# Turning the second FFN's gated tiles with VectorE and a round trip through DRAM instead of TensorE

## The chip, the cores and the metric

The kernel runs on one core of one Trainium2 chip. The metric is the device time of one execution in microseconds (us). Engines are named as in the profile: PE (TensorE), DVE (VectorE), ACT (ScalarE), POOL (GpSimd) and SP (SyncE). SP, POOL and, with the change, ACT issue transfers, which all run on the core's sixteen DMA engines.

## The reference

One layer of a hybrid diffusion backbone with 256 latent and 256 context tokens, D = 2048: a SwiGLU FFN, a token mixer, a second SwiGLU FFN on the latent tokens alone, and a last RMSNorm. The change is in the second FFN:

```
def half_step_ffn(x, mod, i, g, w_up, w_down):
    h = adaln(x, g, mod, i)
    a, b = jnp.split(h @ w_up, 2, axis=-1)
    return x + 0.5 * mod[:, i + 2, None, :] * ((jax.nn.silu(a) * b) @ w_down)

    xl = half_step_ffn(xl, mod_l, 6, g_norm[l, 2], w_ffn2_up[l], w_ffn2_down[l])
return rms_norm(xl, g_final)
```

The hidden width is 5632 = 44 x 128. The kernel works on it in eleven blocks of 512 columns, n = 0 to 10.

## The kernel before

**Precision.** Every matrix product is three fp32r products: each operand is split into a rounded part `hi` (an ACT copy, L128) and the rest `lo` (a DVE subtraction, L129). A weight load of 1 MiB (128 x 2048, fp32) is split in two halves of 1024 columns (`split`, L120). `hi` and `lo` have four buffers each, so two loads are split ahead at most.

**The second FFN's main stage** runs from about 1996 to 2507 us of the profile. Two streams of work are woven by `sequence` (L2242), step by step:

- Steps "s" belong to `quad(n)`, n = 1 to 9. A quad makes one block's gated product, silu(a) * b, by seven products m = 0 to 6 of half the tokens and half the depth (a Strassen form). Each product takes two steps (q = 0, 1) of 12 matmuls. Products write PSUM banks X and Y.
- Steps "u" belong to the stream `units`: first block 10's up products (`up(LAST)`, 8 steps), then the down products of two blocks at a time (`down(n, n+1)`, 8 steps of 24 matmuls).

A quad after the first has 18 steps in this order, which the texts below number 1 to 18: m0 (1, 2), m1 (3, 4), u (5), m2 (6, 7), u (8), m3 (9, 10), m4 (11, 12), u (13), m5 (14, 15), u (16), m6 (17, 18). A step of the quad that follows has a dash: 4' is its fourth step.

**Weights of a quad.** The weights are not all plain loads; some are sums that the DMA engines form. `chain_[q]` is loaded by SP; `first(q)` (at m0) adds another part to it with an accumulating DMA on POOL's queue (`accum`, L740). That sum is what m2 splits at steps 6 and 7. More such sums feed m3 to m6 (`early`, `late_`, `chained`). The accumulation can be issued only when DVE has read the old contents (`lo`, L129). Plain loads go through three buffers `raw`, which SP fills as they come free.

**The gated tiles.** Each quad gives two tiles of 128 tokens x 512 columns: tile 0 in `c12` at the end of step 12, and tile 1 in `c21` at the end of step 18. The down product needs them with the columns on partitions. `wait_turn` puts them in the list `turn`; after each step `turned` (L2044) takes the first of them, if it is at least N_TURN = 2 steps old: four PE transposes through `ident` into a PSUM bank `tr` (L2058), then an ACT copy to `hid2h` (L2061) and a DVE subtraction to `hid2l` (L2063, which turns the sign). The first FFN does it another way (L833 to L845): DVE transposes 32 x 32 blocks, SP stores the tile to DRAM, and later it is fetched back from there in runs of 512 bytes (`hid_load`, L705).

**Order.** The instructions are placed on each engine by a scheduler that follows program order as far as operands are ready; those marked by `keep_in_program_order` (`pinned`) keep their order among themselves. Each engine and each issuing queue then goes through its own list in that order.

**The end.** After the last quad come the down products of blocks 8 and 9 (`down(8, 9)`), then those of block 10 with the last norm (`last2`).

Of the kernel before, what the change touches and what calls it, by code (L numbers as in the profile page):

```python
# [34 lines left out]

N_HID = 3

N_TURN = 2

PACE = (4, 2), (12, 13), (19, 19), (27, 28), (35, 37), (42, 44), (51, 51), (58, 54), (65, 61), (70, 70), (73, 76), (74, 85), (79, 96)  # L40
PACE += (86, 102), (92, 109), (98, 118), (100, 130), (103, 144), (106, 152), (109, 163), (112, 170), (128, 181)
# [17 lines left out]
def tile_layer(ctx: ExitStack, tc: tile.TileContext, I: dict, out: bass.AP):  # L59
# [681 lines left out]
    with pool(name="f1u", bufs=1) as f1u:  # L741
# [91 lines left out]
        def turned():  # L833

            if not turn:
                return
            n, t, ca, spare = turn.pop(0)
            if (n, t) == (NB - 1, 3):
                spare = chp.tile([P, CB], F32, tag="stg", name="stg")
            pinned(nc.vector.transpose(spare, ca))  # L840
            s, tt = divmod(t, 2)
            nc.sync.dma_start(hidd[n][2 * tt + s], spare)
# [1088 lines left out]
    with f2x:  # L1931
        def hid_tiles():

            return [f2.tile([P, FB, T], F32R, tag=g, name=g, bufs=N_HID) for g in ("hid2h", "hid2l")]
# [38 lines left out]
        xTcm.__exit__(None, None, None)  # L1973
        x2cm.__exit__(None, None, None)
        banks.close()
        ps["mm"] = ctx.enter_context(pool(name="ps2", bufs=4, space=PSUM))
        psx = ctx.enter_context(pool(name="psx", bufs=1, space=PSUM))
        ps["tr"] = ctx.enter_context(pool(name="pt2", bufs=2, space=PSUM))
        f2b = f2x.enter_context(pool(name="f2b", bufs=2))

        f3 = ctx.enter_context(pool(name="f3", bufs=1, side="right"))
# [59 lines left out]
        summed = set()  # L2041
        born, clock = {}, [0]

        def turned():  # L2044

            if not turn:
                return
            n, t, sa, sign = turn[0]
            if clock[0] < born[n, t] + N_TURN:
                return  # L2050
            if n not in hids:
                if n - 1 not in hids or len(hids) - len(summed) >= N_HID:
                    return
                hids[n] = hid_tiles()
            turn.pop(0)
            tb = tbank()
            for j in range(FB):
                nc.tensor.transpose(tb[:, j * P : (j + 1) * P], sa[:, j * P : (j + 1) * P], ident)  # L2058
            t3 = tb.rearrange("p (j c) -> p j c", j=FB)
            hh, hl = (x[:, :, t * P : (t + 1) * P] for x in hids[n])  # L2060
            nc.scalar.activation(hh, t3, AF.Copy, scale=sign)  # L2061
            if sign < 0:
                nc.vector.scalar_tensor_tensor(hl, t3, -1.0, hh.bitcast(F32), op0=ALU.mult, op1=ALU.subtract)  # L2063
            else:
                nc.vector.tensor_tensor(hl, t3, hh.bitcast(F32), op=ALU.subtract)
            done.add((n, t))

        done = set()

        def wait_turn(n, t, sa, sign):  # L2070
            turn.append((n, t, sa, sign))
            born[n, t] = clock[0]
            turn.sort(key=lambda x: x[:2])

        def ca_tile():
            return f2b.tile([P, CB], F32, tag="ca", name="ca", bufs=3)

        def quad(n):

            add = lambda o, x, y: nc.vector.tensor_tensor(o, x, y, op=ALU.add)  # L2080
            mul = lambda o, x, y: nc.vector.tensor_tensor(o, x, y, op=ALU.mult)
            B, g = {}, {}

            def p1():
# [25 lines left out]
            def c21():  # L2110
                add(g["a"], B["Y"], g["a"])
                nc.scalar.activation(g["a"], g["a"], AF.Silu)
                mul(g["a"], g["a"], g["y"])
                wait_turn(n, 1, g["a"], -1.0)

            def chained(ab, c):
                return lambda q: accum(chain_[q], part(n, ab, c + q))
# [62 lines left out]
        def up(n):  # L2180

            sab = []
            for ab in range(2):
                bs = [bank() for _ in range(2)]
                for u in range(4):
                    wt = load_split(part(n, ab, u))
                    for j in range(4):
                        k = 4 * u + j
                        w = slice(j * CB, (j + 1) * CB)
                        for t in range(2):  # L2190
                            tt = slice(t * P, (t + 1) * P)
                            mm3(bs[t], h2hi[:, k, tt], h2lo[:, k, tt], *wt(w), k == 0, k == KT - 1)
                    if u == 3:
                        for t in range(2):
                            if ab:
                                nc.vector.tensor_tensor(sab[t], sab[t], bs[t], op=ALU.mult)
                                wait_turn(n, t, sab[t], 1.0)
# [14 lines left out]

        def down(*ns):

            for cb in range(NCB):
                c = slice(cb * CB, (cb + 1) * CB)
                bs = [bank() for _ in range(2)]
                for n in ns:
                    assert (n, 1) in done or not n
                    wt = load_split(I["w_dn2"][n, cb])  # L2220
                    for t in range(2):
                        block(bs[t], n, wt, t, n == ns[0], n == ns[-1])
                    if n == ns[-1]:
                        for t in range(2):
                            a = acc2[:, t, c]
                            if not ns[0]:
                                nc.scalar.activation(a, bs[t], AF.Copy)
                            else:
                                nc.vector.tensor_tensor(a, a, bs[t], op=ALU.add)
                            if n == LAST - 1:  # L2230
                                half_gated(a, a, late["g8"][:, c])
                                accum(a, x2d[t * P : (t + 1) * P, c])
                        if cb == NCB - 1:
                            summed.update(ns)
                    yield

        def units():
            yield from up(LAST)
# [37 lines left out]
        drain(down(LAST - 2, LAST - 1))  # L2276

        def last2():

# [69 lines left out]
def _laid_out(a):  # L2349
# [30 lines left out]
    for n in "12":  # L2380
        up, dn = a[f"w_ffn{n}_up"][0], a[f"w_ffn{n}_down"][0]
        nf = dn.shape[0] // P
        up = up.reshape(KT, P, 2, nf, P)

        rest = up[:, :, :, FB:].reshape(4, 4, P, 2, nf // FB - 1, CB)
        m[f"w_up{n}b"] = asc(rest.transpose(4, 3, 0, 2, 1, 5).reshape(nf // FB - 1, 2, 4, P, 2048))
        first = up[:, :, :, :FB].transpose(3, 2, 1, 0, 4).reshape(-1, 2, P, 2048)
        m[f"w_up{n}"] = asc(first[NPRE:])
        pre = first[:NPRE].reshape(2 * NPRE, P, KT, P)
        loads = []  # L2390
        for k0, k1 in BLOCKS if n == "1" else BLOCKS2:
# [3 lines left out]
        rows = dn.reshape(NF // FB, FB, P, NCB, CB).transpose(0, 3, 2, 1, 4).reshape(NF // FB, NCB, P, 2048)  # L2395
        if n == "1":
            turned = dn.reshape(NF // FB, 4, FB, 32, NCB, CB).transpose(0, 4, 1, 3, 2, 5).reshape(NF // FB, NCB, P, 2048)
            rows = np.concatenate([rows[:1], turned[1:]])
        m[f"w_dn{n}"] = asc(rows)
    w = a["w_in"][0]  # L2400

# [32 lines left out]
```

## Time and profile before

| | us |
|---|---|
| median of 3 runs | 2590.29 |
| the 3 runs | 2586.33, 2590.29, 2592.44 |
| the profiled execution | 2588.91 |
| its span, first to last instruction | 2587.2 |

So 1.7 us of the profiled execution lie outside the span. How to read the profile: the page gives the busy time of each engine and a chain of what released what, followed back from the last instruction. The view of windows gives the busy time of each engine within a stretch, and then the granted PE clock, the mean busy share of the sixteen DMA engines and the rate in GB/s. The view of DMA queues gives, for each queue, packets, megabytes and the time that its packets took as a share of sixteen engines' time in the window; q0 is POOL's queue and q1 holds what SP issues. In a row of the timeline the bracket tells how long the engine sat idle before the instruction, and what it waited for.

### The profile page before, as it was taken

How to read it: one execution, taken by the hardware profiler on the slowest of the kernel's cores; microseconds unless marked ns; L12 is line 12 of the kernel's file. 1: busy time of each engine (PE TensorE's matmuls, PEld its weight loads, DVE VectorE, ACT ScalarE, POOL GpSimd, SP SyncE). 2: the span in 40 equal slices, each digit the busy share in tenths (PEclk: the TensorE clock that was granted, in tenths of full speed). 3: DMA queues.
4: the chain of work that ended last, by engine and by line, in shares of the span. 5: the costliest groups of instructions: out<-in, count | busy, mean ns of one | idle time of the engine just before them, and what ended most of it. 6: DMA issues, size and time to landing. Idle time of an engine off the chain costs nothing. (4 is left out here: it accounts for less than half of the span.)

```text
span 2587.2 us, 33868 instructions
## 1 busy us (share of the span) xinstructions
PE 2555.3 (99%) x12486; PEld 2124.7 (82%) x12486; DVE 2206.6 (85%) x2924; ACT 1405.5 (54%) x1798; POOL 221.9 (9%) x271
## 2 busy tenths in 40 slices
PE   8999999999999999999999999999999999999998
PEld 5788888888887878888889889888898888888886
DVE  7789888888888788888887888898889888898987
ACT  5454444444444455444454347466486676667763
POOL 0000000100010100010110000120000000000001
PEclk8999999999999999999999999999999999999999
DMA  9989999999999999999987897776768999999985
GB/s 392 355 214 275 265 290 277 262 292 281 276 285 282 255 236 246 213 221 231 231 242 268 295 315 242 237 282 212 267 233 246 275 277 283 278 286 278 273 248 171
DMA packets 153478, 684.70 MB, mean 265 GB/s; under 512 B 22872, under 2 KB 43864, under 8 KB 92000
## 3 DMA queue, kind: packets, MB, share of 16 engines
q1 hardware_dynamic: 123936, 490.64, 51.7%
q0 software_dynamic: 29376, 191.90, 37.3%
q8 instruction: 98, 1.61, 0.2%
q14 instruction: 68, 0.56, 0.1%
HBM read 664.59 MB, written 17.89 MB: 264 GB/s over the span
## 5 line engine op out<-in xcount | busy, mean ns | idle before, releaser
L128 ACT ACTIVATE hi<-raw 128x1024 fp32r<-128x1024 f32 (+2 forms) x488 | 504.5, 1040 | 401.2 <-PE mm L152 298.7
L129 DVE TENSOR_TENSOR lo<-raw,hi 128x1024 fp32r<-128x1024 f32 (+2 forms) x476 | 567.2, 1204 | 105.7 <-ACT hi L128 87.4
L128 ACT ACTIVATE hi<-chain 128x1024 fp32r<-128x1024 f32 x352 | 370.1, 1059 | 352.6 <-PE mm L152 199.3
L129 DVE TENSOR_TENSOR lo<-chain,hi 128x1024 fp32r<-128x1024 f32 x352 | 425.2, 1219 | 92.5 <-ACT hi L128 81.2
L152 PE MATMUL mm<-hi,hhi 128*128 128x512 f32 (+3 forms) x1024 | 390.7, 382 | 0.0
L152 PE MATMUL mm<-lo,hhi 128*128 128x512 f32 (+3 forms) x1024 | 387.7, 379 | 1.9 <-DVE lo L129 1.8
L152 PE MATMUL mm<-hi,hlo 128*128 128x512 f32 (+3 forms) x1024 | 386.6, 378 | 0.0
L208 DVE SCALAR_TENSOR_TENSOR junk<-sraw,cBh 128x1024 fp8e5<-128x1024 f32 x192 | 234.3, 1220 | 40.5 <-DMA sraw<-in_w_mt 39.0
L152 PEld LDWEIGHTS mm<-lo,hhi 128*128 128x128 f32 x1024 | 192.8, 188 | 37.0 <-DVE lo L129 4.0
L152 PEld LDWEIGHTS mm<-hi,hlo 128*128 128x128 f32 x1024 | 193.0, 189 | 32.0
L152 PEld LDWEIGHTS mm<-hi,hhi 128*128 128x128 f32 x1024 | 192.9, 188 | 32.2 <-ACT hi L128 0.3
L129 DVE TENSOR_TENSOR lo<-ra,hi 128x1024 fp32r<-128x1024 f32 x104 | 126.2, 1222 | 25.6 <-ACT hi L128 21.7
L128 ACT ACTIVATE hi<-ra 128x1024 fp32r<-128x1024 f32 x104 | 110.1, 1062 | 64.0 <-PE mm L152 34.2
L152 PE MATMUL mm<-lo,hid2h 128*128 128x512 f32 x352 | 137.1, 389 | 0.0
L152 PE MATMUL mm<-hi,hid2h 128*128 128x512 f32 x352 | 137.1, 389 | 0.0
L152 PE MATMUL mm<-hi,hid2l 128*128 128x512 f32 x352 | 137.0, 389 | 0.0
L152 PE MATMUL mm<-hi,sumshl 128*128 128x512 f32 x400 | 123.2, 389 | 0.0
L208 DVE SCALAR_TENSOR_TENSOR sr<-sr,cBl 128x1024 f32<-128x1024 f32 x84 | 102.1, 1222 | 16.4 <-DMA sr<-in_w_mt 15.1
L740 POOL DMA_DIRECT2D chain<-in_w_up1b x60 | 53.1, 886 | 724.1 <-DVE lo L129 583.9
L152 PE MATMUL mm<-hi,sumshh 128*128 128x512 f32 x352 | 108.3, 389 | 0.0
L152 PE MATMUL mm<-hhi,hi 128*128 128x512 f32 (+1 forms) x288 | 101.4, 352 | 0.0
L152 PE MATMUL mm<-hhi,lo 128*128 128x512 f32 (+1 forms) x288 | 99.0, 344 | 0.0
(490 smaller groups left out, 5415.1 us busy)
## 6 DMA issues: line engine op xcount, KB each, us to landing
raw<-in_w_dn SPq DMA_DIRECT2D x70, 1024.0 KB, 10.0
chain<-in_w_up1b POOLq DMA_DIRECT2D x60, 1024.0 KB, 10.7
sraw<-in_w_mt SPq DMA_DIRECT2D x96, 512.0 KB, 8.4
sr<-in_w_mt SPq DMA_DIRECT2D x81, 512.0 KB, 5.7
raw<-in_w_up1b SPq DMA_DIRECT2D x40, 1024.0 KB, 9.1
mraw<-in_w_m SPq DMA_DIRECT2D x32, 1024.0 KB, 7.6
chain<-in_w_dn POOLq DMA_DIRECT2D x30, 1024.0 KB, 10.2
chain<-in_w_up2b POOLq DMA_DIRECT2D x28, 1024.0 KB, 11.4
```

The lines of the kernel that those rows point to most:

```text
L128: scalar[0].activation(hi, src, AF.Copy)
L129: vector[0].tensor_tensor(lo, src, hi.bitcast(F32), op=ALU.subtract)
L152: tensor[0].matmul(out_ap, s, m, start=first and not n, stop=last and n == 2, skip_group_check=skip)
L208: ins = nc.vector.scalar_tensor_tensor(junk() if junk else raw, raw, 1.0, cB[s], op0=ALU.mult, op1=ALU.mult, accum_out=mT[:, i, s, kt, h : ...
L740: accum = lambda dst, src: nc.gpsimd.dma_start(dst, src, accum_op=ALU.add)
```

## The change

The tiles of blocks 1 to 9 are no longer transposed by PE. The gating now includes the sign (one `scalar_tensor_tensor`). At the end of the same step DVE transposes the tile's 32 x 32 blocks into a spare tile (`g["b"]` or `g["y"]`, N_TURN = 1). One step later ACT's queue stores it to DRAM (256 KB, rows of 2 KB). Six and seven steps after the transpose ACT's queue fetches it back into the old tile, in four transfers of 64 KB made of runs of 512 bytes, two transfers in each of the two steps. Ten steps after the transpose ACT copies it to `hid2h` and DVE subtracts to `hid2l` (`halves`). So tile 0 (step 12) is stored at 13, fetched at 18 and 1', and split at 4'. Tile 1 (step 18) is stored at 1', fetched at 6' and 7', and split at 10'. Store, fetch and split are pinned.

The rows of `w_dn2` are permuted on the host to fit the order in which the columns now lie. Block 10's two tiles still go through PE. `down` now goes through two column blocks at once, block n first and then n + 1, so that the later tiles are needed two units later; it holds four PSUM banks, and the pool `mm` has six banks instead of four with two for `tr`. `ca` has four buffers instead of three. After the last quad the first two units of `down(8, 9)` are put between the store, the fetches and the split of the last tile.

```diff
-N_TURN = 2
+N_TURN = 1
+N_STORE = 1
+N_FETCH = 6
+N_MOVE = 10
...
-        ps["mm"] = ctx.enter_context(pool(name="ps2", bufs=4, space=PSUM))
+        ps["mm"] = ctx.enter_context(pool(name="ps2", bufs=6, space=PSUM))
...
-        ps["tr"] = ctx.enter_context(pool(name="pt2", bufs=2, space=PSUM))
...
+        hid2d = {n: dr.tile([2, P, CB], F32, name=f"hid2{n}") for n in QUADS}
...
+        def halves(n, t, x, runs=False):
+            hh, hl = (y[:, :, t * P : (t + 1) * P] for y in hids[n])
+            if runs:
+                hh, hl = (y.rearrange("p j (a c) -> p a j c", c=32) for y in (hh, hl))
+            pinned(nc.scalar.activation(hh, x, AF.Copy))
+            pinned(nc.vector.tensor_tensor(hl, x, hh.bitcast(F32), op=ALU.subtract))
...
-            for j in range(FB):
-                nc.tensor.transpose(tb[:, j * P : (j + 1) * P], sa[:, j * P : (j + 1) * P], ident)
...
+            if spare is not None:
+                turn.pop(0)
+                nc.vector.transpose(spare, sa)
+                moved.append((clock[0], n, t, sa, spare))
...
+        def stored(n, t, sa, spare):
+            pinned(nc.scalar.dma_start(hid2d[n][t], spare))
+
+        def fetched(n, t, sa, spare, bands):
+            rows = hid2d[n][t].rearrange("(a r) (b x) -> b r a x", a=4, b=4)
+            for b in bands:
+                pinned(nc.scalar.dma_start(sa[32 * b : 32 * b + 32].rearrange("r (a x) -> r a x", a=4), rows[b]))
+
+        def arrived():
+            for then, *x in moved:
+                age = clock[0] - then
+                if age == N_STORE:
+                    stored(*x)
+                elif age in (N_FETCH, N_FETCH + 1):
+                    b = 2 * (age - N_FETCH)
+                    fetched(*x, (b, b + 1))
+            if moved and clock[0] >= moved[0][0] + N_MOVE and room(moved[0][1]):
+                _, n, t, sa, _ = moved.pop(0)
+                halves(n, t, sa.rearrange("p (a j c) -> p a j c", a=4, j=FB), True)
...
-                mul(g["a"], g["a"], g["b"])
-                wait_turn(n, 0, g["a"], -1.0)
+                negative(g["a"], g["b"])
+                wait_turn(n, 0, g["a"], g["b"])
...
-            for cb in range(NCB):
+            for c0 in (0, 2):
...
                 for n in ns:
+                    for cb in (c0, c0 + 1):
...
+        before_final()
+        final = down(LAST - 2, LAST - 1)
+        for gap, more in ((N_STORE, True), (N_FETCH - N_STORE, False), (1, True)):
+            clock[0] += gap
+            arrived()
+            if more:
+                next(final)
+        while moved:
+            clock[0] += N_MOVE
+            arrived()
         while turn:
-            clock[0] += 1
             turned()
-        before_final()
-        drain(down(LAST - 2, LAST - 1))
+        drain(final)
```

More of the change, by code (lines that the diff above doesn't have):

```diff
@@ L2042, in tile_layer, with room @@
         born, clock = {}, [0]
+        hid2d = {n: dr.tile([2, P, CB], F32, name=f"hid2{n}") for n in QUADS}
+        moved = []
+        def room(n):
+            if n not in hids:
+                if n - 1 not in hids or len(hids) - len(summed) >= N_HID:
+                    return False
+                hids[n] = hid_tiles()
+            return True
+        def halves(n, t, x, runs=False):
[4 more added lines that the diff above has]
+            pinned(nc.vector.tensor_tensor(hl, x, hh.bitcast(F32), op=ALU.subtract))
+            done.add((n, t))
         def turned():
@@ L2047, in turned @@
                 return
-            n, t, sa, sign = turn[0]
+            n, t, sa, spare = turn[0]
             if clock[0] < born[n, t] + N_TURN:
                 return
[L2051 to L2056, printed above, removed]
-            for j in range(FB):
-                nc.tensor.transpose(tb[:, j * P : (j + 1) * P], sa[:, j * P : (j + 1) * P], ident)
@@ L2059, in turned @@
[L2059 to L2066, printed above, removed]
+            if spare is not None:
+                turn.pop(0)
+                nc.vector.transpose(spare, sa)
+                moved.append((clock[0], n, t, sa, spare))
+            elif room(n):
+                turn.pop(0)
+                tb = bank()
+                for j in range(FB):
+                    nc.tensor.transpose(tb[:, j * P : (j + 1) * P], sa[:, j * P : (j + 1) * P], ident)
+                halves(n, t, tb.rearrange("p (j c) -> p j c", j=FB))
@@ L2068, in tile_layer, with wait_turn @@
         done = set()
-        def wait_turn(n, t, sa, sign):
-            turn.append((n, t, sa, sign))
+        def wait_turn(n, t, sa, spare):
+            turn.append((n, t, sa, spare))
             born[n, t] = clock[0]
@@ L2075, in ca_tile @@
         def ca_tile():
-            return f2b.tile([P, CB], F32, tag="ca", name="ca", bufs=3)
+            return f2b.tile([P, CB], F32, tag="ca", name="ca", bufs=4)
         def quad(n):
             add = lambda o, x, y: nc.vector.tensor_tensor(o, x, y, op=ALU.add)
-            mul = lambda o, x, y: nc.vector.tensor_tensor(o, x, y, op=ALU.mult)
+            negative = lambda o, y: nc.vector.scalar_tensor_tensor(o, o, -1.0, y, op0=ALU.mult, op1=ALU.mult)
             B, g = {}, {}
@@ L2112, in c21 @@
                 nc.scalar.activation(g["a"], g["a"], AF.Silu)
-                mul(g["a"], g["a"], g["y"])
-                wait_turn(n, 1, g["a"], -1.0)
+                negative(g["a"], g["y"])
+                wait_turn(n, 1, g["a"], g["y"])
             def chained(ab, c):
@@ L2196, in up @@
                                 nc.vector.tensor_tensor(sab[t], sab[t], bs[t], op=ALU.mult)
-                                wait_turn(n, t, sab[t], 1.0)
+                                wait_turn(n, t, sab[t], None)
                             else:
@@ L2213, in down @@
         def down(*ns):
-            for cb in range(NCB):
-                c = slice(cb * CB, (cb + 1) * CB)
-                bs = [bank() for _ in range(2)]
+            for c0 in (0, 2):
+                bs = {}
                 for n in ns:
[L2219 to L2223, printed above, removed]
-                        for t in range(2):
[L2225 to L2235, printed above, removed]
+                    for cb in (c0, c0 + 1):
+                        assert (n, 1) in done or not n
+                        c = slice(cb * CB, (cb + 1) * CB)
+                        if n == ns[0]:
+                            bs[cb] = [bank() for _ in range(2)]
+                        wt = load_split(I["w_dn2"][n, cb])
+                        for t in range(2):
+                            block(bs[cb][t], n, wt, t, n == ns[0], n == ns[-1])
+                        if n == ns[-1]:
+                            for t in range(2):
+                                a = acc2[:, t, c]
+                                if not ns[0]:
+                                    nc.scalar.activation(a, bs[cb][t], AF.Copy)
+                                else:
+                                    nc.vector.tensor_tensor(a, a, bs[cb][t], op=ALU.add)
+                                if n == LAST - 1:
+                                    half_gated(a, a, late["g8"][:, c])
+                                    accum(a, x2d[t * P : (t + 1) * P, c])
+                            if cb == NCB - 1:
+                                summed.update(ns)
+                        yield
         def units():
@@ L2271, in tile_layer @@
             assert next(x, x) is x
+        before_final()
[7 more added lines that the diff above has]
+            clock[0] += N_MOVE
+            arrived()
         while turn:
-            clock[0] += 1
             turned()
-        before_final()
-        drain(down(LAST - 2, LAST - 1))
+        drain(final)
         def last2():
@@ L2395, in _laid_out @@
         rows = dn.reshape(NF // FB, FB, P, NCB, CB).transpose(0, 3, 2, 1, 4).reshape(NF // FB, NCB, P, 2048)
+        turned = dn.reshape(NF // FB, 4, FB, 32, NCB, CB).transpose(0, 4, 1, 3, 2, 5).reshape(NF // FB, NCB, P, 2048)
         if n == "1":
-            turned = dn.reshape(NF // FB, 4, FB, 32, NCB, CB).transpose(0, 4, 1, 3, 2, 5).reshape(NF // FB, NCB, P, 2048)
             rows = np.concatenate([rows[:1], turned[1:]])
+        else:
+            rows = np.concatenate([rows[:1], turned[1:-1], rows[-1:]])
         m[f"w_dn{n}"] = asc(rows)
```

## The prediction

> **What bounds the kernel now.** I read the page first, then the windows of the changed stage, then the chain of waits inside one quad.
>
> ```profile
> span 2587.2 us, 33868 instructions
> PE 2555.3 (99%) x12486; PEld 2124.7 (82%) x12486; DVE 2206.6 (85%) x2924; ACT 1405.5 (54%) x1798; POOL 221.9 (9%) x271
> ...
> 1996.00:2507.00 511.00, 510.46 (x2282) 421.28 (x2282) 446.86 (x424) 352.17 (x373) 41.89 (x48) 1.00 0.94 276
> ```
>
> PE is never idle for long, but the last row says more: in the second FFN's 511 us DVE is busy 87%, ACT 69%, and the DMA engines 0.94 of the time. So the question is not only what PE saves but what the other three have left. The chain through one quad, from step 16 to m2 of the next:
>
> ```profile
> 2255.57 5.45 PE mm L152 x24
> 2261.02 0.44 PE tr L2058 x4
> 2261.46 5.45 PE Y L152 x24
> 2266.91 4.53 PE X L152 x20
> 2271.45 0.49 PE tr L2058 x4
> 2271.94 0.92 PE X L152 x4
> 2272.86 5.44 PE Y L152 x24
> 2278.30 5.44 PE mm L152 x24
> 2283.74 5.44 PE Y L152 x24
> ```
>
> PE runs without a hole; 24 matmuls take 5.44 us, and a group of four transposes 0.44 to 0.49. A quad has 14 x 12 + 4 x 24 = 264 matmuls, 59.84 us, and two groups: 60.8 us. Now the DMA engines, in a pattern that comes back with each quad:
>
> ```profile
> 2225.00:2231.00 6.00, 5.47 (x25) 4.20 (x24) 6.00 (x6) 3.80 (x5) 0.00 (x0) 1.00 0.22 51
> 2231.00:2286.00 55.00, 55.00 (x248) 45.47 (x247) 48.58 (x48) 38.24 (x40) 5.26 (x6) 1.00 1.01 296
> 2286.00:2291.00 5.00, 5.00 (x24) 4.14 (x23) 5.00 (x5) 3.72 (x5) 0.00 (x0) 1.00 0.21 88
> ```
>
> They work for 55 us on end (share 1.01, records overlap a little) and then rest for some 4 to 4.7 us (5 x 0.79, 6 x 0.78). The rest begins when the sum for m2 has landed. What that landing means for PE:
>
> ```profile
> 2216.67 5.44 PE mm L152 x24
> ...
> 2228.37 5.44 PE mm L152 x24
> ...
> 2222.41 2.01 ACT L128 ACTIVATE hi<-chain 128x1024 fp32r<-128x1024 f32 x2 [3.70 <-DMA chain<-in_w_up2b]
> ...
> 2283.09 2.01 ACT L128 ACTIVATE hi<-ra 128x1024 fp32r<-128x1024 f32 x2 [2.75 <-DMA ra<-in_w_up2b]
> ...
> 2266.96 0.88 POOL L740 DMA_DIRECT2D ra<-in_w_up2b  x1 [24.30 <-DVE lo L129]
> ...
> 2269.83 0.88 POOL L740 DMA_DIRECT2D ra<-in_w_up2b  x1 [1.99 <-DVE lo L129]
> ```
>
> In these two quads ACT stands 3.70 and 2.75 us at step 7 until the second accumulation of `first` is there. In the first, ACT starts 0.30 us after m2 was due (2216.67 + 5.44 = 2222.11), and m2 takes 6.26 us instead of 5.44: PE loses 0.82. In the second it starts 0.65 us before m2 and PE loses nothing. The point is thus near 0.5 us before m2, and **the slack is 0.1 to 0.4 us**. The kernel is bound by PE with the DMA engines right behind it, at one place of each quad.
>
> **The change part by part.**
>
> ```profile
> L2058 PE MATMUL tr<-ident,ca x72: 270/272/304, 2000.3 to 2514.6; 128*128 128x128 f32 x72
> L2061 ACT ACTIVATE hid2h<-tr x20: 578/585/602, 2001.3 to 2515.4; 128x512 fp32r<-128x512 f32 x20
> L2063 DVE SCALAR_TENSOR_TENSOR hid2l<-tr,hid2h x18: 683/684/694, 2002.6 to 2515.5; 128x512 fp32r<-128x512 f32 x18
> L840 DVE STREAM_TRANSPOSE c<-ca x20: 691/704/711, 208.3 to 922.5; 128x512 f32<-128x512 f32 x20
> L2081 DVE TENSOR_TENSOR ca<-ca 128x512 f32<-128x512 f32 x9 | 6.2, 684 | 0.0
> L845 DVE SCALAR_TENSOR_TENSOR ca<-ca,c x20: 649/686/692, 207.6 to 902.4; 128x512 f32<-128x512 f32 x20
> L842 SPq DMA_DIRECT2D hid<-c x20: 326/327/1792, 209.1 to 923.2; - x20
> DMA to landing us min/median/max: 3.7/7.6/12.5
> L711 SPq DMA_DIRECT2D hidl<-hid x20: 303/572/17456, 879.1 to 1162.9; - x20
> DMA to landing us min/median/max: 3.2/7.2/28.8
> ```
>
> *PE.* 18 groups go (72 transposes), in the path, at 0.44 to 0.49: **-8.4 us** with 0.465. Block 10's two groups stay.
>
> *DVE.* The sign moves into the gating (686 for 684 ns) and the split keeps its kind (684): nothing. New are 18 transposes of 0.704 us, 1.4 per quad. They lie beside PE: DVE has 64 of 511 us free, 7.6 per quad, and the old `hid2l` leaves the crowded steps after the gating as the transpose enters them. Cost 0; without that cover, at most 12.7.
>
> *ACT.* The split's copy stays (0.585). Ninety DMA issues are new. No row shows one on ACT's queue; on SP they take 0.327, on POOL 0.88 (rows above), so 29 us, with bounds 0 and 79, against 159 us that ACT has free. I take 0 on the path, as SP's kind is the nearest. What matters is that ACT stands still when an issue or the split waits: behind it on ACT are the `hi` copies, for them `lo`, and for that PE.
>
> *DMA engines.* Prices come from the view of DMA queues, first for this stage, then for the first FFN's tiles:
>
> ```profile
> DMA packets 19329, 140.88 MB, mean 276 GB/s; under 512 B 2151, under 2 KB 2151, under 8 KB 2151
> q0 software_dynamic: 7203, 52.39, 51.7%
> q1 hardware_dynamic: 12095, 88.09, 42.2%
> ...
> q0 software_dynamic: 386, 2.77, 95.0%
> q1 hardware_dynamic: 384, 0.20, 6.7%
> ...
> q1 hardware_dynamic: 3746, 1.86, 114.7%
> ```
>
> The first three rows (1996 to 2507) hold only 8 KB packets beside tiny ones. Accumulating: 0.517 x 511 us for 50 MiB, 5.3 us a MiB; each engine has 8 packets of one MiB, so 0.66 us a packet. Plain: 0.422 x 511 for 84 MiB, 2.57 us a MiB, 0.32 a packet. The last row (950 to 958, 512-byte fetches alone) gives 8 x 16 / 3746 = 0.034 us a packet. A fetched tile is 512 such packets, 32 for each engine: 1.1 us. A stored tile is 8 packets of 2 KB for each engine: between 8 x 0.034 and 8 x 0.32, 0.3 to 2.6; I take a quarter of the 8 KB price, 0.65, as the sizes scale so. Two tiles: **3.5 us more DMA work in each quad**, which rests about 4.
>
> *Where it falls.* Tile 0's store (13) and fetch (18, 1') and tile 1's store (1') all lie in the 55 us before the sum for m2 lands. The pair of rows of 886 to 900 us shows how the queues share: 386 accumulating packets of 8 KB and 384 plain ones of 512 bytes in the same time, turn by turn, one for one. So the sum's 16 packets per engine always get their turn, 16 x 0.66 = 10.6 us alone; from the end of the first issue (2267.84) to 2283.09 it took 15.25, so others had some 4 us and landing the rest. With ACT's queue and SP's both full at each turn a turn is 0.66 + 0.32 + 0.03 to 0.08: 16.2 to 17.0 us, plus landing. That is 0.9 (if the 15.25 holds no landing time) to 2.9 us later; I take 2.0, between them. PE comes to m2 earlier by 0.49 (tile 1's group lay in that stretch). Less 0.2 slack: PE waits **2.3 us**.
>
> *The wait that is new.* Tile 0's split stands on ACT at 4', three steps, about 8.2 us, behind its second pair of fetches, and these queue behind the first: 32 packets at one a turn, when a turn is 1.0 us while the sum is loaded. They can hardly land before the sum, and may land 3 us after. ACT then holds back m2's second `hi` copies, with the split itself (0.59) ahead of them. I take 0.9 us more (bounds 0 and 3): **3.2 us per quad**, bounds 1.2 and 5.7.
>
> *How many quads.* Eight transitions carry a tile over. Before, the first two showed no such wait of ACT (rows of this kind begin at 2160 us), so I count seven: 7 x 3.2 = **+22.4 us**.
>
> *The end.*
>
> ```profile
> 2511.01 3.40 PE mm L152 x15
> 2514.41 0.90 PE tr L2058 x8
> ```
>
> Today the last tile's gating hides under matmuls of block 8. Then: from 2511.01 to the gating's end 3.1 us, transpose 0.7, store 0.33 + 3.7 to 7.6, four issues 1.3 and fetch 3.2 to 7.2, split 0.6: 13 to 21 us, against two units (10.9) and block 10's groups (0.9) for cover. **+2.5 us** (0 to 9), near the low end, as little else loads there.
>
> Sum: 2588.9 - 8.4 + 22.4 + 2.5 = **2605.4**. The profiled execution lies 1.4 us below the median of 2590.29, within the runs' 2586.33 to 2592.44; I leave it at that and say 2605.
>
> **The rule of the skill.** The Trainium skill (DMA: Bandwidth & Descriptors, Queues, rings and completion order) says that an engine takes a whole packet of some 9 to 17 descriptors from one ring before it turns to the next. By that the fetch of a band, 8 descriptors for each engine, would pass in one turn and not in eight. The rows of 886 to 900 speak against it, since there each 512-byte piece waited for its own turn; no run here shows ACT's ring.
>
> **The rivals.**
>
> *Faster, hidden.* If ACT's small pieces slip through at the start, before the sum's turns begin, and the rest of 4 us takes the delay up, PE keeps its gain. This decides at one place: does tile 0's second fetch land within the 8.2 us before its split? The fetch's least landing time of 3.2 us speaks for it, the 28.8 against. 2588.9 - 8.4 + 2 = 2582.5. Chance 0.22.
>
> *Balanced.* The sum comes 0.9 later and the fetch lands with it: 0.9 + 0.49 - 0.2 = 1.2 us per quad, seven times 8.4, which is just the gain, and 1 to 2.5 at the end: 2591. Chance 0.14.
>
> *Whole bands in one turn.* The fetch is through early, ACT isn't held, and only the sum's delay of 2.3 is left: 2588.9 - 8.4 + 16.1 + 2.5 = 2599. The rule of the Trainium skill above would lead here. Chance 0.12.
>
> *DMA becomes the bound throughout.* The rest of 4.2 us can't be used, because it ends only when PE's steps free buffers; then a quad takes 60.8 x 0.94 + 3.5 + 4.2 = 64.9, 4.1 more, eight times 33, and the end's 2.5: 2625. Chance 0.12.
>
> **How the numbers follow.** Forecast 2605, its own span 2600 to 2615, chance 0.40. About 0.2% (5 us) is what a measurement of this kernel can tell from no change. Faster 0.22 (hidden), same 0.14 (balanced), slower 0.64 (forecast, bands, bound throughout). The range 2581 to 2624 leaves out the slowest half of the last case, the bounds above 4.5 us per quad, and the hidden case with a free end.
>
> **What would show it.** Right: no `tr<-ident,ca` row, quads of about 63 us, with PE's holes at m2 and nowhere else; ACT waiting there for the tile's fetch and for the sum; DMA share at 0.97 or more in the stage; a fetch landing after 10 us or more. Wrong: quads of 59.9 us with fetches landed in 5 us (hidden), or holes at other products (DVE late, for which no row speaks). If a DMA issue on ACT took far more than 0.33 us, holes would follow each fetch step, and my cost for ACT would be the step that failed.

## The result, and the profile after

| | us |
|---|---|
| before, median of 4 runs | 2590.56 (2586.33 to 2592.44) |
| after, median of 4 runs | 2659.33 (2653.32 to 2662.66) |
| ratio after to before, 95% interval | 1.0265 (1.0242 to 1.0288) |
| profiled execution of after | 2653.32, span 2651.6 |

The kernel is slower by 69 us. The sign was forecast, the size was not: 2605 was said, with a range up to 2624. First the head of after's page:

```profile
span 2651.6 us, 33877 instructions
PE 2571.3 (97%) x12414; PEld 2127.4 (80%) x12414; DVE 2214.7 (84%) x2942; ACT 1399.2 (53%) x1798; POOL 220.9 (8%) x271
```

The 72 transposes are gone from PE (12486 instructions before, 12414 now), and DVE has 18 more. Yet the span is 64 us longer, and PE's busy time has grown by 16 us. The view of windows of after, over the second FFN's main stage and some 30 us behind it:

```profile
1996.00:2600.00 604.00, 550.60 (x2320) 443.51 (x2319) 472.39 (x461) 358.36 (x387) 43.52 (x50) 0.95 0.87 257
```

PE, which had no hole to speak of (510 of 511 us), is idle for 53 us. The DMA engines are *less* busy than before, 0.87 for 0.94, although they move more. So something stands still and holds both back. The chain of after through one quad (start, length, what) names it:

```profile
2160.26 18.66 DMA hid<-cy
2178.95 0.31 ACTq L2092
...
2179.87 0.59 ACT hid2h L2064
...
2182.23 1.23 DVE lo L135
...
2183.50 4.63 PE Y L158 x10
2188.13 5.94 PE mm L158 x24
2194.07 5.44 PE Y L158 x24
...
2231.09 18.71 DMA hid<-cy
2249.82 0.31 ACTq L2092
```

From one store of a tile 1 (`hid<-cy`) to the next are 70.83 us, a quad that took 60.8 before. The store's 18.7 us are in the chain whole: the store lands, ACT issues a fetch (L2092), splits tile 0 (L2064), DVE makes a `lo`, and only then does PE run on.

The chain shows a second price. Behind the hole ten matmuls take 4.63 us, where 24 take 5.44 elsewhere. Windows of after around this hole (PE's busy time and matmuls come first, the granted PE clock is the third number from the end):

```profile
2176.00:2181.00 5.00, 0.00 (x0) 0.00 (x0) 0.52 (x1) 1.70 (x3) 0.00 (x0) 0.78 0.44 173
2181.00:2188.00 7.00, 5.72 (x13) 4.04 (x14) 7.00 (x8) 4.55 (x6) 0.00 (x0) 0.50 0.10 16
```

While PE stands, the granted clock falls to 0.50, and it stays there for a while after PE has resumed: 13 matmuls take 5.72 us, 0.44 each instead of 0.23. The same is seen at seven holes of 5 to 8 us, and the mean granted clock is 0.984 to 0.987 in all four executions of after, for 0.995 in the profiled one of before. In slices of 0.5 us, the busy time multiplied by what the clock lacks adds up to 19.5 us, an estimate. With it the account of the profiled execution closes: 52.9 us more of holes and 19.5 of slower matmuls, less the 8.4 of the transposes, are 64.0, and the span grew by 64.4. So more than a quarter of the loss is not waiting, but the slower clock behind long waits.

ACT's timeline of after shows where ACT stood:

```profile
2231.09 0.34 ACTq L2087 DMA_DIRECT2D hid<-cy  x1
...
2237.20 2.01 ACT L134 ACTIVATE hi<-chain 128x1024 fp32r<-128x1024 f32 x2 [0.32 <-DMA chain<-in_w_up2b]
2249.82 0.31 ACTq L2092 DMA_DIRECT2D ca<-hid  x1
2250.18 0.63 ACT L2129 ACTIVATE ca<-ca 128x512 f32<-128x512 f32 x1 [10.97 <-DMA hid<-cy]
2250.36 0.31 ACTq L2092 DMA_DIRECT2D ca<-hid  x1
2250.71 0.61 ACT L2064 ACTIVATE hid2h<-ca 128x512 fp32r<-128x512 f32 x1
2251.23 1.99 ACT L134 ACTIVATE hi<-chain 128x1024 fp32r<-128x1024 f32 x2
```

At 2237.20 the first half of m2's sum is split, early enough. Next in ACT's list is tile 1's **first fetch** (2249.82), which needs tile 1's store to have landed. ACT takes its list in order, so the silu of step 4', tile 0's split and m2's second half (2251.23) stand behind it for 11 us. The store had been issued at 2231.09, just 8 us of ACT's list ahead. The bracket is on the silu, because an issue has no row of waiting of its own. The view of waits of after counts it:

```profile
ACT ca L2129 <- DMA hid<-cy: 74.6, 7, 11.3
...
PEld Y L158 <- ACT hi L134: 48.5, 9, 8.3
...
ACT hi L134 <- DMA chain<-in_w_up2b: 15.6, 9, 4.2
```

Seven times, 10.7 us each. The wait for the sum itself (last row; 4.2 us more are on `ra`), which I had taken for the one that decides, is smaller than in the kernel before, whose waits for sums are:

```profile
ACT hi L128 <- DMA chain<-in_w_up2b: 20.6, 8, 3.9
ACT hi L128 <- DMA ra<-in_w_up2b: 11.5, 5, 2.8
```

The view of DMA issues of after (size, median us to landing) says how late the store is:

```profile
ca<-hid ACTq DMA_DIRECT2D x72, 64.0 KB, 6.5
hid<-ca ACTq DMA_DIRECT2D x9, 256.0 KB, 11.1
hid<-cy ACTq DMA_DIRECT2D x9, 256.0 KB, 18.1
```

### The profile page after: what moved, and what is told of

It reads as the page before. It is cut to its first block, busy times and chain, and to the rows that moved or that the text cites. A ratio compares the mean times of both kernels' runs of the same rounds, so it can differ in the third digit from the quotient of the medians.

```text
span 2651.6 us, 33877 instructions
## 1 busy us (share of the span) xinstructions
PE 2571.3 (97%) x12414; PEld 2127.4 (80%) x12414; DVE 2214.7 (84%) x2942; ACT 1399.2 (53%) x1798; POOL 220.9 (8%) x271
```

## The experiments

Theory A, from these rows: tile 1's store lies in ACT's ring behind tile 0's fetch pieces, lands late, and ACT stands at tile 1's first fetch. Rival B: the added traffic delays m2's sum, as I had forecast. Times are compared by the ratio to the kernel before on the same chip, with its 95% interval.

**1. Fetch from an input, so that no fetch waits for a store.**

```diff
-            rows = hid2d[n][t].rearrange("(a r) (b x) -> b r a x", a=4, b=4)
+            rows = I["x"][:P, :CB].rearrange("(a r) (b x) -> b r a x", a=4, b=4)
```

> The eight band fetches of each block take their 512-byte pieces from the input x (first 128 rows, first 512 columns) and not from hid2; stores, fetches, splits and their places stay, so DMA traffic and instruction counts are those of after. The splits of blocks 1 to 9 so work on other numbers. Theory A (ACT stands, in order, at tile 1's first fetch until tile 1's store has landed, 10.5 us in each of seven quads): that wait is gone, 2580 to 2605 us, no wait of ACT on hid<-cy. Rival B (the added DMA traffic delays m2's sum, whatever the fetch waits for): stays near 2650. If the step of my prediction (tile 0's split held by its own late fetch, 3.2 us per quad) is real beside A, it shows here as some 2605; if not, 2582 to 2590.

2626.45 us, 1.0133 (1.0104 to 1.0162). Half of the loss is gone and half is left, which neither theory had said. The wait on `hid<-cy` is gone; another stands in its place. Waits, then chain:

```profile
ACT hid2h L2064 <- DMA ca<-in_x: 60.0, 9, 7.1
```

```profile
2227.29 18.82 DMA ca<-in_x
...
2246.22 0.64 ACT hid2h L2064
...
2249.90 4.14 PE Y L158 x10
```

Now tile 0's split waits for tile 0's own second pair of fetches, 18.82 us under way. That is the wait which the prediction had named, and far longer than it said.

**2. Leave out stores and fetches; the split reads the tile unturned.**

```diff
-                if age == N_STORE:
-                    stored(*x)
-                elif age in (N_FETCH, N_FETCH + 1):
-                    b = 2 * (age - N_FETCH)
-                    fetched(*x, (b, b + 1))
+                pass
```

> Store and fetches are left out; the splits of blocks 1 to 9 work on the tile as gated, not turned. The DVE transposes, the splits' places, the order of the down products and the six banks stay. Theories A and B (both in the transfers): about 2582 us, the 8.4 us of PE transposes gained. Rivals C (down's new order and banks) or D (DVE transposes in the crowded steps): above 2600, with PE's holes at m2 still there.

2590.83 us, 0.9989 (0.9979 to 1.0). So all 69 us come from the transfers and the waits for them, not from DVE or from the new order of the down products. But PE's 8.4 us are not gained either. Without transfers the kernel is only 2.8 us (0 to 5.4) better than before.

**3. The store on SP's queue.**

```diff
-            pinned(nc.scalar.dma_start(hid2d[n][t], spare))
+            nc.sync.dma_start(hid2d[n][t], spare)
```

> The two stores of a block are issued by SP's queue among the weight loads, not by ACT's; all else as in after. Theory A with its detail (tile 1's store lands 18.1 us after issue because it lies behind tile 0's 32 fetch pieces per engine in ACT's own ring): the store lands in 4 to 10 us, the wait at m2 shrinks from 10.5 to 0 to 4 us, 2585 to 2612 us. If the store is slow for the load on the DMA engines and not for the ring, it lands in 15 us or more here too and the time stays above 2640. Rival B: near 2650.

2630.67 us, 1.0145 (1.013 to 1.016). The store now lands in good time, and ACT's wait for it all but goes, in the view of that line:

```profile
  ACT ca L2129: 9.7, 4
  ACT hid2h L2064: 3.4, 1
...
DMA to landing us min/median/max: 4.9/10.6/14.2
```

What is left, beside the traffic itself, is again tile 0's split behind its own fetch (34.7 us in nine waits). Theory A holds for the store, and explains half of the loss.

**4. Tile 0 not fetched.**

```diff
-                elif age in (N_FETCH, N_FETCH + 1):
+                elif age in (N_FETCH, N_FETCH + 1) and x[1]:
```

> Tile 0's four fetches of each block are left out, so its split works on old numbers; tile 0's store, tile 1's store, fetch and all else stay. Theory A with its detail: tile 1's store has nothing ahead of it in ACT's ring and lands in 5 to 10 us, m2's hole shrinks from 10.5 to 0 to 4 us, 2583 to 2612 us. If the store's 18.1 us come from SP's and POOL's load alone: stays above 2640. Rival B with half the fetch traffic gone: about 2620.

2626.5 us, 1.0127 (1.011 to 1.0144), more than theory A had said. The same view here:

```profile
  ACT ca L2129: 48.2, 7
```

and its view of DMA issues:

```profile
hid<-cy ACTq DMA_DIRECT2D x8, 256.0 KB, 11.8
```

With nothing of tile 0 ahead of it tile 1's store lands in 11.8 us instead of 18.1. So the ring accounts for a part only, and 11.8 us is still too late for a fetch that stands 8 us behind: ACT waits 6.9 us each time.

**5. Fetch in rows of 2 KB: same bytes, a quarter of the packets.**

```diff
-                pinned(nc.scalar.dma_start(sa[32 * b : 32 * b + 32].rearrange("r (a x) -> r a x", a=4), rows[b]))
+                pinned(nc.scalar.dma_start(sa[32 * b : 32 * b + 32], hid2d[n][t][32 * b : 32 * b + 32]))
```

> Each band fetch takes 32 whole rows of 2 KB of hid2 (rows 32b to 32b + 31) and not 128 pieces of 512 bytes: same bytes, same four issues on ACT, same waits, 8 packets per engine and tile in place of 32; the splits of blocks 1 to 9 so get their columns in another order. Theory A2 (each packet in ACT's ring waits for a turn against SP's and POOL's, some 0.75 us each while both are full, so 32 pieces take 19 to 24 us, hold tile 0's split and put tile 1's store behind them): fetch of tile 0 lands in 5 to 11 us, tile 1's store in under 13, m2's hole falls from 9.5 to 0 to 4 us per quad, 2590 to 2618 us. Rival B (the bytes moved, or the store's wait alone, set the hole): above 2630.

2612.22 us, 1.0066 (1.0045 to 1.0087). By the view of DMA issues of this kernel, tile 1's store now lands in 11.4 us:

```profile
ca<-hid ACTq DMA_DIRECT2D x60, 64.0 KB, 5.6
hid<-cy ACTq DMA_DIRECT2D x8, 256.0 KB, 11.4
```

Three quarters of the loss go with the number of packets alone. Only the size of the pieces was changed, so it is their number that made both waits long. That each waits for a turn of its own is inferred, from counts of packets that the last section gives.

**6. Is PE the bound at all? The kernel before, without its transposes.**

```diff
-            tb = tbank()
-            for j in range(FB):
-                nc.tensor.transpose(tb[:, j * P : (j + 1) * P], sa[:, j * P : (j + 1) * P], ident)
-            t3 = tb.rearrange("p (j c) -> p j c", j=FB)
+            if n < LAST:
+                t3 = sa.rearrange("p (j c) -> p j c", j=FB)
...
```

> The kernel before with PE's transposes of blocks 1 to 9 left out: the split reads the gated tile from SBUF, unturned; down's order, banks and ages are those of before. Theory L (the stage is already held by a loop without PE's transposes in it: sum landed, m2's split on ACT and DVE, raw buffers free, SP's next loads, some 54 us of DMA work on end, next sum): no gain, 2587 to 2593 us, with new holes at m2 of 0.7 to 1.5 us. Rival (PE is the bound, as my prediction had it, and the 7 us that no_move lost come from down's new order): 2582 to 2584.

2591.2 us, 0.9998 (0.9986 to 1.001): nothing gained. Windows of the kernel before and then of this one:

```profile
2080.00:2540.00 460.00, 459.46 (x2057) 379.06 (x2056) 402.66 (x387) 312.45 (x330) 40.15 (x46) 1.00 0.93 271
```

```profile
2080.00:2540.00 460.00, 454.20 (x1991) 371.68 (x1991) 400.73 (x387) 307.94 (x330) 39.18 (x45) 1.00 0.92 272
```

What PE saves turns up in the main as 5.8 us of holes. Theory L: the stage was already held by a loop with no transpose in it: m2's sum lands, ACT and DVE split it, buffers come free, SP and POOL load on for some 55 us without a pause, and the next sum lands.

**7. Down's new order alone, with PE turning the tiles.**

```diff
-N_TURN = 1
+N_TURN = 2
...
-                wait_turn(n, 0, g["a"], g["b"])
+                wait_turn(n, 0, g["a"], None)
...
-                wait_turn(n, 1, g["a"], g["y"])
+                wait_turn(n, 1, g["a"], None)
```

> After with the turning given back to PE: tiles of blocks 1 to 9 go through four PE transposes again (two steps after the gating, into a bank of the pool of six), no DVE transposes, stores or fetches; w_dn2's rows in the old order; the sign in the gating, four ca buffers and down's new order stay. Theory L: the time of before, 2587 to 2594 us. Rival C (down's new order and the shared banks cost what no_move didn't gain): 2597 to 2600.

2594.44 us, 1.0009 (0.9995 to 1.0023): the same as before. Order and banks are not the cause.

**8. The fetches in the rest behind the sum.** Ages 13 (tile 0) and 8 (tile 1) for all four bands, splits at 15 and 11; the last transfers behind the last quad are put in a like order.

```diff
-                elif age in (N_FETCH, N_FETCH + 1):
-                    b = 2 * (age - N_FETCH)
-                    fetched(*x, (b, b + 1))
+                elif age == (13, 8)[x[1]]:
+                    fetched(*x, range(4))
```

> Same transfers as after, placed apart for the two tiles: tile 0 is stored at step 13 as before but all four bands are fetched 13 steps after the transpose (step 7', behind m2's sum, where the DMA engines rest) and split at 9'; tile 1 is stored at 1', fetched at 8' and split at 11'. So nothing lies ahead of tile 1's store in ACT's ring and no wait for a fetch stands on ACT before m2's split. Theories A2 and L together: m2's hole falls to that of no_move, 2588 to 2598 us, no gain over before. If the pieces cost a turn each there too, against SP's loads, tile 0's split stands and holes of 1 to 3 us appear at m3 or step 8': 2600 to 2620. Rival B (traffic as such): 2605 or more, hole still at m2.

2617.35 us, 1.009 (1.007 to 1.0111), not the 2588 to 2598 of the two theories, but in the range of rival B. The waits for the tiles shrink to 11.4 us, and the bands land in 4.6 us (median; 6.5 in after), but the waits for the sums grow, from 20.6 and 11.5 us in the kernel before to:

```profile
ACT hi L134 <- DMA chain<-in_w_up2b: 33.9, 13, 4.5
ACT hi L134 <- DMA ra<-in_w_up2b: 27.7, 9, 5.4
ACT hid2h L2064 <- DMA ca<-hid: 11.4, 4, 3.2
```

The rest is no free room. My reading is that ACT and DVE then free the buffers from which the loads start again; this run doesn't show it.

**9. The traffic alone.** As 1, and tile 0's split reads the spare tile, so ACT waits for no transfer of tile 0. The order of ACT's list is that of after.

```diff
-                _, n, t, sa, _ = moved.pop(0)
-                halves(n, t, sa.rearrange("p (a j c) -> p a j c", a=4, j=FB), True)
+                _, n, t, sa, spare = moved.pop(0)
+                x = sa if t else spare
+                halves(n, t, x.rearrange("p (a j c) -> p a j c", a=4, j=FB), True)
```

> As the run that fetched from the input x (stores, fetches and their places on ACT as in after), and tile 0's split reads the spare tile, so no split of tile 0 and no fetch of tile 1 waits on ACT for a transfer; the splits of blocks 1 to 9 work on other numbers. Theory L with the added DMA work (3.4 us per quad by the 5.3% of the ACT queue in the run with the fetches behind the sum): 2610 to 2618 us, ACT at m2 waits for the sum alone. If DMA work as such costs nothing and all the rest was ACT standing: 2591, the time without transfers.

2612.73 us, 1.0072 (1.0051 to 1.0093), as theory L had said. ACT now waits for the sums:

```profile
ACT hi L134 <- DMA ra<-in_w_up2b: 39.9, 13, 5.2
ACT hi L134 <- DMA chain<-in_w_up2b: 34.9, 12, 5.1
```

ACT's queue takes this share of the DMA engines (queue, packets, MB, share, from 2080 to 2540 us):

```profile
q10 hardware_dynamic: 10649, 7.67, 5.4%
```

That is 24.8 us in 460, or 3.4 us of DMA time in a quad of some 63 us.

**10 to 12. The same with room in the loop.** Half of each `w_dn2` load is left out, in three kernels: before, number 2 and number 8.

```diff
-        raw = raw_tile(n)
-        nc.sync.dma_start(raw, src)
-        wt = split(raw, n)
+        raw = raw_tile(n)
+        if same:
+            nc.sync.dma_start(raw[:, :1024], src[:, :1024])
...
-                        wt = load_split(I["w_dn2"][n, cb])
+                        wt = load_split(I["w_dn2"][n, cb], same=True)
```

> The kernel before with half of each w_dn2 load left out (1024 of 2048 columns fetched, used twice by the split), which takes 4 x 0.5 MiB x 2.57 = 5.1 us of DMA work out of each quad; all else stays, PE's transposes too. Theory L adds: freed of the DMA loop, the kernel is held by PE alone, quads of 60.3 to 60.9 us, 2585 to 2590 us. If something else holds it: the same quads and holes as before.

> The run without store and fetch, with half of each w_dn2 load left out in addition. Theory L: with the DMA loop relieved PE's saved 8.4 us show at last, quads of 59.9 to 60.1 us, 2579 to 2584 us. If the saving was lost elsewhere (DVE, ACT, the order of down): 2588 to 2591 as with the full loads.

> The kernel with the fetches behind the sum (13 and 8 steps after the transposes), with half of each w_dn2 load left out in addition. Theory L: 3.4 us of DMA work added and 5.1 taken away, so the DMA loop is shorter than before's and the transfers are hidden: 2580 to 2588 us, against 2617 with the full loads. If the ACT queue's issues and waits for the tiles cost in their own right: 2600 or more.

Before with half the loads: 2590.51 us, 0.9991 (0.9978 to 1.0004). Without transfers: 2583.3 us, 0.996 (0.9945 to 0.9976). Their windows, in this order:

```profile
2080.00:2540.00 460.00, 460.00 (x2063) 380.13 (x2062) 403.83 (x388) 314.67 (x332) 40.05 (x46) 1.00 0.85 232
```

```profile
2080.00:2540.00 460.00, 460.00 (x2035) 380.92 (x2034) 412.23 (x405) 314.82 (x331) 39.20 (x45) 1.00 0.86 233
```

Both fill PE to the last microsecond, and now the transposes are worth 0.31% or 8.0 us (ratios 0.9991 and 0.996; by their intervals some 5 us more or less), as the 8.4 that I had counted. So theory L holds in this: with the full loads it is DMA work that keeps PE from its gain. That the freeing of buffers closes the loop is not shown by these runs. The third kernel took 2601.95 us, 1.0033 (1.0023 to 1.0044), where theory L had 2580 to 2588 and the other case 2600 or more. Fetches in the rest cost something even where the DMA engines have time.

**13 to 15. What the traffic's price consists of.** Number 9 with half the `w_dn2` loads; number 9 with 2 KB rows as in 5; and after with tile 0's split moved to 9', tile 1's bands fetched together at 8' and split at 11':

```diff
-                elif age == (13, 8)[x[1]]:
-                    fetched(*x, range(4))
+                elif not x[1] and age in (N_FETCH, N_FETCH + 1):
+                    b = 2 * (age - N_FETCH)
+                    fetched(*x, (b, b + 1))
+                elif x[1] and age == 8:
+                    fetched(*x, range(4))
```

(This diff is against number 8.)

> The run with traffic alone (fetches from the input x into tiles that no split of tile 0 waits for), with half of each w_dn2 load left out in addition. If the 22 us are DMA work in a loop without slack: 5.1 us per quad are freed against 3.4 added, so they vanish: 2580 to 2587 us, quads of 59.9 to 60.3. If they are turns that the sum's packets lose, whatever room there is: 2595 to 2603, ACT still waiting for the sum at m2.

> The run with traffic alone, each band fetched as 32 rows of 2 KB of the input x in place of 128 pieces of 512 bytes: same bytes, a quarter of the packets. If the 22 us go with bytes and DMA time: 2608 to 2614 us. If they go with the number of packets (turns): 2595 to 2604.

> Stores and tile 0's fetches stay where they are in after (13, 18, 1' and 1'); tile 0's split goes from 4' to 9', tile 1's four bands are fetched together at 8' and split at 11'. So the transfers fall beside the loads, and the waits of ACT for them go. If the ladder is right: the time of the traffic alone, 2606 to 2618 us, no ACT wait on hid<-cy or ca<-hid over 1 us per quad. If a wait only moves: 2625 or more.

Traffic with half the loads: 2590.02 us, 0.998 (0.9968 to 0.9992), between the two expectations. Against the same kernel without transfers (0.996) the traffic costs 0.2%, 5 us, instead of 0.83%, 21.5 us; three quarters of its price is the lack of room among the loads. Traffic in 2 KB rows: 2615.08 us, 1.0077 (1.0055 to 1.01), no different from 512-byte pieces within the intervals. So the price of the traffic goes with bytes, and only the *lateness* of a tile goes with the number of packets. The late split: 2625.36 us, 1.0114 (1.0093 to 1.0135), worse than the traffic alone by 11 us. That is the 2625 or more that was expected if a wait only moves, though ACT waits for the tiles just once, 3.3 us in all, by its waits:

```profile
ACT hi L134 <- DMA chain<-in_w_up2b: 41.0, 12, 5.6
ACT hi L134 <- DMA ra<-in_w_up2b: 37.2, 13, 5.5
ACT hid2h L2064 <- DMA ca<-hid: 3.3, 1, 3.3
PEld Y L158 <- DVE lo L135: 35.5, 51, 1.2
```

The last row is PE waiting for DVE's `lo` in many small pieces; in run 9 it is 25.4 us. Both kernels that use the steps after m2 for fetches and splits (8 and this one) lose there. I take it that ACT's and DVE's extra work delays the refill of the buffers, but no run isolates it; that stays open. No kernel among these that does the whole work beats the kernel before.

## Why the prediction was wrong, by its steps

The runs make a ladder. Each rung takes the difference of two ratios, times 2590.6; the intervals leave some 3 to 10 us on each.

| step | forecast, us | measured, us | from |
|---|---|---|---|
| PE's groups gone | -8.4 | -2.8 | no transfers against before |
| sum for m2 later by DMA work | 7 x 2.3 = 16.1 | 21.5 | traffic alone against no transfers (1.0072 - 0.9989) |
| tile 0's split behind its own fetch | 7 x 0.9 = 6.3 | 15.8 | fetch from input against traffic alone (1.0133 - 1.0072) |
| tile 1's fetch behind its store | not priced | 34.2 | after against fetch from input (1.0265 - 1.0133) |
| the end | 2.5 | no hole of PE | window 2560 to 2600 us of after |

The four rungs add to 68.7. The lower two hold the holes and also the slower matmuls behind them: the clock of 0.50 is seen in after and in run 1 (some 18 us lost in the latter's profiled execution, its slowest), and not in run 9, whose longest hole is some 1.1 us. They are sizes in this order of removal: the two waits of ACT lie one over the other, so that with the store out of the way first (run 3) 31 us go, and with tile 0's fetch left out (run 4) 36.

- **The step that failed** is "Where it falls" together with "The wait that is new". The text counted tile 1's store as load on the DMA engines and stopped there. It said that ACT stands when "an issue or the split waits", and then followed only the split. Tile 1's first fetch is an issue that waits, it stands on ACT ahead of tile 0's split and of m2's second half, and it cost 34 of the 69 us in the order of the ladder. A landing time of 3.7 to 7.6 us, taken from the first FFN's stores, was used for the end alone; 18.1 us were measured here.
- **What a hole costs** was put at its length. The runs show more where it is long: the granted clock of 0.50 behind seven holes of after adds some 2.8 us to each (19.5 / 7). The prediction has no term for it, though it is nearly as large as all the waits that it counted (22.4).
- **Tile 0's split**: the mechanism was right, and the runs fit the form of the reckoning, a piece a turn. The term was mis-sized, 0.9 us for a quad where some 2 were lost (15.8 / 8). The text let the fetch land with the sum or 3 us after; run 1 shows ACT still 6.8 us at that split, with the fetch 18.8 us under way, and part of the 15.8 us is the slower clock.
- **DMA work** was right: 3.4 us per quad for the 3.5 forecast, and 0.31 to 0.44 us for an issue on ACT (medians of the kernels) for the 0.327 assumed. Its effect was larger than forecast, more so as the 2.3 us held 0.49 for PE's earlier arrival, and the upper bound of 2.9 us for the delay doesn't follow from the 17.0 us beside it (17.0 - 15.25 = 1.75). The rival in which the rest of 4 us can't be used, priced at 4.1 us per quad, came nearest for this term: 21.5 / 8 = 2.7 us per quad by run 9. Its reason, that the rest ends only when buffers come free, no run isolates.
- **PE's gain** was counted in full, with 0.49 us a quad taken back at m2, although the text itself put the slack at m2 at 0.1 to 0.4 us. With so little slack a saving outside the loop can't be gained; run 6 shows that it isn't.
- **DVE** at nothing was right: transposes of 0.70 and 0.71 us, a split of 0.69, and no loss in run 2.
- **The end**, put at 2.5 us, cost PE nothing that the trace shows: in after PE is busy for all of the 40 us from 2560 to 2600 us, in which the last tile is stored, fetched and split.
- Of what the text wanted to see, holes at m2 and late fetches came; quads of 63 us (70.8 in the chain above) and "DMA share at 0.97 or more" did not. The share fell to 0.87; in run 9, where ACT doesn't stand for the tiles, it is 0.96, so a standing ACT keeps the DMA engines waiting too.

The prediction weighed a rule of the Trainium skill (DMA: Bandwidth & Descriptors, Queues, rings and completion order) by which a band would pass in one turn. Run 5 speaks against it in ACT's ring: with a quarter of the pieces, and the same bytes, tile 1's store came down from 18.1 to 11.4 us, and so do the counts of packets in the last section. The same page (Two DMAs through the same engine are not ordered) says that within one queue of one engine descriptors start in order. The trace agrees, as far as landing times tell: the store of tile 1 landed after 18.1 us behind tile 0's pieces, and in 11.8 without them.

## What to carry to other kernels

A transfer issued from a compute engine's queue puts its wait into that engine's list: for each new issue ask what it waits for, how far ahead in the same list that was started, and what stands behind it, not only how long the issue takes. Before a saving on one engine is counted, look whether the loop that ends at the next wait contains it; with 0.1 to 0.4 us of slack against the DMA engines, 8.4 us of PE were worth nothing. A regular pause of the DMA engines is not room by itself: transfers put into it (run 8) cost as much as beside the loads. And price a long hole of PE by more than its length: look at the granted clock behind it.

## What the runs showed of the hardware

Small pieces in one queue are slow while the others are loading, though they take next to no DMA time. The view of DMA queues of after, from 2223 to 2250 us (packets, MB, share), with the issues and their median landing:

```profile
q1 hardware_dynamic: 829, 6.01, 53.2%
q0 software_dynamic: 288, 2.10, 37.3%
q10 hardware_dynamic: 720, 0.52, 6.4%
...
ca<-hid ACTq DMA_DIRECT2D x5, 64.0 KB, 13.5
hid<-cy ACTq DMA_DIRECT2D x1, 256.0 KB, 18.7
```

ACT's ring (q10) moved 720 packets, 45 for each of 16 engines, in 27 us: some 0.6 us for each, an estimate, and about one for each packet of SP's queue (829 / 16 = 52), against 27 x 0.064 / 45 = 0.038 us that one occupies an engine. A 256 KB store, which landed in 3.7 to 12.5 us in the first FFN, took 18.1 us in this queue (median).

The granted PE clock went with PE's holes. In after it falls to 0.50 when PE has stood for some 3 to 4.5 us, and comes back to 1.00 some 5 to 8 us after PE has resumed, at each of the seven long holes. In run 9, with many short holes, it stays at 1.00 throughout the stage.
